# Row-wise infinity norm of an 8192x8192 matrix: issuing the loads from GpSimd instead of SP

## The chip, the cores and the metric

The kernel runs on one core of a Trainium2 chip. The metric is the device time of one execution in microseconds (us), as the median of several executions. A separate execution is taken with the hardware profiler; its views (busy times, waits, the chain of work that ended last, the timeline, DMA issues) are what the argument is read from.

The engines that matter here are VectorE (DVE), which does nearly all of the arithmetic, ScalarE (ACT) and GpSimd (POOL), which help with the last rows, and SyncE (SP), which in the kernel before does nothing but issue DMAs. "SPq" in a view is SP's instruction queue, where the DMA-issuing instructions stand.

## The reference

```python
def setup_inputs():
    return {"x": np.random.randn(8192, 8192).astype(np.float32)}

def reference(x):
    return np.linalg.norm(x, ord=np.inf, axis=1)
```

NumPy takes `axis=1` as "a vector norm for each row", so the result is, for each of the 8192 rows, the largest absolute value in it: 8192 floats. The input is 268.4 MB and is read exactly once; the output is 32 KB.

## The kernel before

**Tiling.** The 8192 rows are spread over the 128 partitions, 64 rows (R = 64) to a partition. `GROUPS = [46, 18]` (line 18) makes two groups, so that in the first each partition holds 46 neighbouring rows and in the second 18; within a group, what a partition reads is contiguous in memory. The work of a partition is therefore one long line of 64 x 8192 elements, which is cut into loads by column widths (lines 21 to 26): two loads of 8192 elements per partition (one row each, 4 MiB over all partitions), twenty-nine of 16384 (two rows, 8 MiB), one more of 16384 and one of 8192 that are shared out among engines, and then the last row in six pieces of 3920, 1984, 1040, 576, 320 and 352 elements. That is 33 entries in `WHOLE` and 6 in `LAST`, 39 loads in all.

**Buffers.** All loads but the very last go into one ring (line 54) of 3 x 16384 elements a partition, that is, three loads of full size. `load` (line 97) takes the next place in the ring, going back to 0 when the piece would not fit. So load u lies where load u-3 lay, and its DMA has to wait until the reduces that read load u-3 are done. By this rule the last full-size load (u = 31) lies in the ring where load 28 lay, and the load of 8192 together with the first five pieces of the last row lies where load 29 lay. The last piece has a buffer of its own, `last` (line 58), which also has columns for the partial results of the other pieces. The test on line 110 drops, for part of the loads, a dependency on the earlier load in the same place, which the reduce in between orders already; the change leaves it as it is.

**Engines.** `absmax` (line 67) is a VectorE reduce with absolute value; for a load of two rows it gives two results a partition at once. `shared` (line 85) splits a piece: VectorE reduces the first part, while ScalarE takes the absolute value of the rest in place and GpSimd reduces it as 32-bit integers (`max_pool`, line 72). It is used for the second row of load 31, for load 32 and for the first five pieces of the last row. At the end VectorE reduces `last`, pieces and partial results together (line 153), and SP stores the last column of results (line 154); ScalarE's queue stores the others (line 159).

**Order.** `keep` holds the instructions of an engine in the order in which the program gives them. Each engine has one in-order queue. In the kernel before every load is issued from SP's queue:

```python
        inst = nc.sync.dma_start(out=buf, in_=x_of[first[row]][:, a : a + w]).ins
```

SP has no other work until the last store, so what stands behind a load that waits for its place in the ring is only the next load. The program asks for each load just ahead of its use:

```python
    for u, (w, g) in enumerate(WHOLE):
        buf = load(pos, w)
```

SP however runs ahead of the other engines as far as the ring lets it: while load u is being reduced, loads u+1 and u+2 are already issued.

Of the kernel before, what the change touches and what calls it, by code (L numbers as in the profile page):

```python
# [1 line left out]

# [4 lines left out]

P = 128
FP32 = mybir.dt.float32
INT32 = mybir.dt.int32  # L10
MAX = mybir.AluOpType.max
X = mybir.AxisListType.X
ABS = mybir.ActivationFunctionType.Abs

GROUPS = [46, 18]


WHOLE = (
    [(8192, ())] * 2 + [(16384, ())] * 29 + [(16384, (3712, 3680)), (8192, (2016, 1984))]
)
LAST = [
    (3920, (1680,)), (1984, (848,)), (1040, (432,)), (576, (240,)), (320, ()), (352, ())
]
RING = 3 * 16384


@with_exitstack  # L30
def kernel(
    ctx: ExitStack,
    tc: tile.TileContext,
    x: bass.AP,
    out: bass.AP,
):
    nc = tc.nc
    n_rows, n_cols = x.shape
    R = n_rows // P
    assert R == sum(GROUPS) and n_cols == 8192  # L40
    keep = tc.keep_in_program_order


    first = []
    x_of, out_of = {}, {}
    for k in GROUPS:
        f = len(first)
        x_of[f] = x[f * P : (f + k) * P].rearrange("(p r) m -> p (r m)", r=k)
        out_of[f] = out[f * P : (f + k) * P].rearrange("(p r) -> p r", r=k)
        first += [f] * k  # L50

    single = ctx.enter_context(tc.tile_pool(name="single", bufs=1))

    ring = single.tile([P, RING], FP32)
    res = single.tile([P, R], FP32)

    n_parts = sum(1 + len(g) for w, g in LAST[:-1])
    last = single.tile([P, LAST[-1][0] + n_parts], FP32)

    def not_before(inst, other, why):  # L60
        tc.add_manual_dep(
            inst.ins, other.ins.name,
            mybir.DependencyInfo(mybir.DependencyClass.Sync, mybir.DependencyReason.DATA),
            reason=why,
        )

    def absmax(dst, src):
        return keep(nc.vector.tensor_reduce(  # L68
            out=dst, in_=src, axis=X, op=MAX, apply_absolute_value=True,
        ))  # L70

    def max_pool(dst, src):

        pool = nc.gpsimd
        keep(pool.add_instruction(  # L75
            mybir.InstTensorReduce(
                name=nc.get_next_instruction_name(),
                ins=[pool.lower_ap(src.bitcast(INT32))],
                outs=[pool.lower_ap(dst.bitcast(INT32))],
                op=MAX,  # L80
                axis=X,
            )
        ))

    def shared(part, buf, g):

        a = buf.shape[1] - sum(g)
        red = absmax(part[:, :1], buf[:, :a])
        for i, c in enumerate(g):
            keep(nc.scalar.activation(buf[:, a : a + c], buf[:, a : a + c], ABS))  # L90
            max_pool(part[:, 1 + i : 2 + i], buf[:, a : a + c])
            a += c
        return red

    loads = []

    def load(pos, w):

        row = pos // n_cols
        a = pos - first[row] * n_cols  # L100
        if pos + w == R * n_cols:
            buf = last[:, :w]
        else:
            at = loads[-1][0] + loads[-1][1] if loads else 0
            if at + w > RING:
                at = 0
            buf = ring[:, at : at + w]
        inst = nc.sync.dma_start(out=buf, in_=x_of[first[row]][:, a : a + w]).ins  # L108
        if pos + w < R * n_cols:
            if (len(loads) + 4) % 10 < 5:  # L110


                for b, v, earlier in loads:
                    if b < at + w and at < b + v:
                        tc.declare_no_dep(
                            inst, earlier, reason="ordered by the reduces in between",
                        )
            loads.append((at, w, inst))
        return buf


    pos = 0
    for u, (w, g) in enumerate(WHOLE):
        buf = load(pos, w)
        row, k = pos // n_cols, w // n_cols
        pos += w
        whole = k - 1 if g else k
        if whole:
            red = absmax(
                res[:, row : row + whole],  # L130
                buf[:, : whole * n_cols].rearrange("p (c m) -> p c m", m=n_cols),
            )
        if g:
            part = single.tile([P, 1 + len(g)], FP32, name=f"part{u}")
            shared(part, buf[:, whole * n_cols :], g)
            max_pool(res[:, row + whole : row + k], part)
        if u == 1:

            not_before(
                keep(nc.scalar.activation(res[:, :1], res[:, :1], ABS)),  # L140
                red, "not before the second row is in",
            )


    n = LAST[-1][0]
    for h, (w, g) in enumerate(LAST[:-1]):
        buf = load(pos, w)
        pos += w
        shared(last[:, n : n + 1 + len(g)], buf, g)
        n += 1 + len(g)  # L150

    load(pos, LAST[-1][0])
    absmax(res[:, R - 1 :], last)
    final = nc.sync.dma_start(out=out_of[first[-1]][:, GROUPS[-1] - 1 :], in_=res[:, R - 1 :])


    for f, o in out_of.items():
        k = min(o.shape[1], R - 1 - f)
        early = keep(nc.scalar.dma_start(out=o[:, :k], in_=res[:, f : f + k]))
        tc.add_manual_dep(  # L160
            early.ins, final.ins.name,
            mybir.DependencyInfo(
                mybir.DependencyClass.NoSync, mybir.DependencyReason.SCHED_ONLY
            ),
            reason="takes the later semaphore",
        )


# [1 line left out]
_INS = ['x']  # L170
_OUTS = [((8192,), 'float32')]


# [23 lines left out]
```

## Time and profile before

| | |
|---|---|
| Median of 5 executions | 627.45 us (627.35 to 627.52) |
| The profiled execution's own time | 627.55 us |
| Its span, first to last instruction | 625.8 us |
| VectorE busy | 536.7 us in 40 instructions |
| ScalarE busy | 15.0 us in 10 |
| GpSimd busy | 14.1 us in 14 |
| HBM read | 268.44 MB, 429 GB/s over the span |

The span counts from the first to the last instruction of the core; 1.75 us of the execution's own time lie outside it. Busy times leave out the instructions that issue DMAs. An engine's idle time is listed with what ended it (`<-`). "us to landing" is the time from the instruction that issues a DMA to the arrival of its last semaphore update, so it includes the time that the DMA stood behind earlier ones. "ring<-in_x_dram" is a load into the ring, "res" the tile of results, "part" and "last" the tiles of partial results. The lines of the profile stand in the prediction.

### The profile page before, as it was taken

The numbers are of one execution on the slowest core, as the hardware profiler recorded it, in microseconds if no ns is written. First come the engines' busy times: TensorE is split into PE (matmuls) and PEld (weight loads), VectorE is DVE, ScalarE is ACT, GpSimd is POOL, SyncE is SP. The second block draws the span as 40 slices with busy tenths as digits, with TensorE's granted clock in tenths as the row PEclk, the third lists the DMA queues.
The fourth block names the chain that finished last, engine by engine and source line by source line (L and its number), as shares of the span: only waits on it lengthen the run. The fifth ranks groups of instructions, "written<-read, shape, count | busy, mean of one in ns | idle before, by whom it ended". The sixth has DMA issues, their size and how long they took to land.

```text
span 625.8 us, 175 instructions
## 1 busy us (share of the span) xinstructions
DVE 536.7 (86%) x40; ACT 15.0 (2%) x10; POOL 14.1 (2%) x14
## 2 busy tenths in 40 slices
DVE  1938988889888899888898888988889888899888
ACT  0000000000000000000000000000000000000044
POOL 0000000000000000000000000000000000000026
DMA  8999999999999999999999999999999999999997
GB/s 369 436 469 402 469 402 469 402 469 402 469 402 448 423 415 457 402 469 402 469 402 469 402 469 402 469 402 461 411 423 448 406 465 402 469 402 469 402 436 304
DMA packets 6049, 268.47 MB, mean 429 GB/s; under 512 B 1057, under 2 KB 1313, under 8 KB 1697
## 3 DMA queue, kind: packets, MB, share of 16 engines
q1 hardware_dynamic: 5760, 268.44, 99.3%
q10 hardware_dynamic: 288, 0.03, 0.0%
q14 instruction: 1, 0.00, 0.0%
HBM read 268.44 MB, written 0.03 MB: 429 GB/s over the span
## 4 chain that ended last, share of the span: by engine, by line
DMA 71%; DVE 28%; SPq 0%; issue 0%; DVEq 0%
DMA ring<-in_x_dram 71%; DVE res L68 28%; DVE last L68 1%; SPq L108 0%; DVEq L68 0%
## 5 line engine op out<-in xcount | busy, mean ns | idle before, releaser
L68 DVE TENSOR_REDUCE res<-ring 128x2 f32<-128x16384 f32 (+1 forms) x32 | 525.4, 16420 | 86.4 <-DMA ring<-in_x_dram 86.4
L90 ACT ACTIVATE ring<-ring 128x3712 f32<-128x3712 f32 (+7 forms) x8 | 13.6, 1719 | 577.3 <-DMA ring<-in_x_dram 574.0
L75 POOL TENSOR_REDUCE part<-ring 128x1 int32<-128x3712 int32 (+3 forms) x4 | 10.1, 2561 | 607.7 <-ACT ring L90 607.7
L68 DVE TENSOR_REDUCE part<-ring 128x1 f32<-128x800 f32 (+1 forms) x2 | 5.5, 2748 | 0.1
L68 DVE TENSOR_REDUCE last<-ring 128x1 f32<-128x2240 f32 (+4 forms) x5 | 5.3, 1117 | 0.2 <-DMA ring<-in_x_dram 0.2
L75 POOL TENSOR_REDUCE last<-ring 128x1 int32<-128x1680 int32 (+3 forms) x4 | 3.4, 854 | 0.6 <-ACT ring L90 0.4
L140 ACT ACT_TABLE_LOAD x1 | 1.3, 1283 | 0.7 <-PEq L181 0.7
L140 ACT ACTIVATE res<-res 128x1 f32<-128x1 f32 x1 | 0.2, 203 | 29.3 <-DVE res L68 29.3
L68 DVE TENSOR_REDUCE res<-last 128x1 f32<-128x361 f32 x1 | 0.5, 530 | 0.1
L75 POOL TENSOR_REDUCE res<-part 128x1 int32<-128x3 int32 x2 | 0.4, 197 | 0.1
L181 POOL MEMSET const-float32-0.0<- 128x1 f32 x1 | 0.1, 98 | 0.2 <-issue 0.2
L181 POOL MEMSET const-uint8-127<- 128x1 uint8 x1 | 0.1, 102 | 0.0
L181 POOL MEMSET const-bfloat16-1.0<- 128x1 bf16 x1 | 0.1, 101 | 0.0
L181 POOL MEMSET const-float32-1.0<- 128x1 f32 x1 | 0.1, 98 | 0.0
## 6 DMA issues: line engine op xcount, KB each, us to landing
ring<-in_x_dram SPq DMA_DIRECT2D x3, 4096.0 KB, 21.4
ring<-in_x_dram SPq DMA_DIRECT2D x1, 1960.0 KB, 35.5
ring<-in_x_dram SPq DMA_DIRECT2D x1, 992.0 KB, 37.4
ring<-in_x_dram SPq DMA_DIRECT2D x1, 520.0 KB, 38.2
ring<-in_x_dram SPq DMA_DIRECT2D x30, 40.8
ring<-in_x_dram SPq DMA_DIRECT2D x1, 288.0 KB, 38.4
last<-in_x_dram SPq DMA_DIRECT2D x1, 176.0 KB, 38.3
ring<-in_x_dram SPq DMA_DIRECT2D x1, 160.0 KB, 38.4
```

Source lines behind the costliest of these rows:

```text
L68: return keep(nc.vector.tensor_reduce(out=dst, in_=src, axis=X, op=MAX, apply_absolute_value=True,))
L75: keep(pool.add_instruction(mybir.InstTensorReduce(name=nc.get_next_instruction_name(), ins=[pool.lower_ap(src.bitcast(INT32))], outs=[poo ...
L90: keep(nc.scalar.activation(buf[:, a : a + c], buf[:, a : a + c], ABS))
L140: keep(nc.scalar.activation(res[:, :1], res[:, :1], ABS)),
L181: nc = _bacc.Bacc("TRN2", target_bir_lowering=False, num_devices=1)
```

## The change

Only the first load stays on SP. All others, 38 DMAs, are issued from GpSimd's queue, with `keep`, so that they stand in the program's order among GpSimd's own instructions. The loads are asked for through `load_up_to`: during the two-row loads one at a time, as before; from the first entry that is shared among engines (u = 31, whose `g` is not empty) all that are left are asked for at once, so that they stand in GpSimd's queue ahead of its first reduce. Widths, ring places, reduces, the split among engines and the stores are the same.

```diff
-        inst = nc.sync.dma_start(out=buf, in_=x_of[first[row]][:, a : a + w]).ins
+        queue = nc.gpsimd if loads else nc.sync
+        inst = keep(queue.dma_start(out=buf, in_=x_of[first[row]][:, a : a + w])).ins
...
+    widths = [w for w, _ in WHOLE + LAST]
+    bufs = []
+
+    def load_up_to(n):
+        while len(bufs) < n:
+            bufs.append(load(sum(widths[: len(bufs)]), widths[len(bufs)]))
+
+
     pos = 0
     for u, (w, g) in enumerate(WHOLE):
-        buf = load(pos, w)
+        load_up_to(len(widths) if g else u + 1)
+        buf = bufs[u]
...
-    for h, (w, g) in enumerate(LAST[:-1]):
-        buf = load(pos, w)
-        pos += w
+    for buf, (w, g) in zip(bufs[len(WHOLE) :], LAST[:-1]):
         shared(last[:, n : n + 1 + len(g)], buf, g)
         n += 1 + len(g)
 
-    load(pos, LAST[-1][0])
     absmax(res[:, R - 1 :], last)
```

## The prediction, made before the change was run

> **What bounds the kernel now.** I read first the page's strip of 40 slices, its count of packets and its table of DMA queues, because the kernel reads 268 MB and does little with it.
>
> ```profile
> DVE  1938988889888899888898888988889888899888
> ...
> DMA  8999999999999999999999999999999999999997
> ...
> DMA packets 6049, 268.47 MB, mean 429 GB/s; under 512 B 1057, under 2 KB 1313, under 8 KB 1697
> ...
> q1 hardware_dynamic: 5760, 268.44, 99.3%
> ```
>
> The DMA engines are busy in every slice but the first and the last, and the packets of one queue, SP's, fill 99.3% of the time of 16 engines. VectorE has about a tenth of its time free. The 5760 packets tell the shape of a descriptor: 39 loads of 128 data packets and 16 semaphore writes are 5616, and the last store adds 144. So a row of a two-row load goes as one packet of 64 KB.
>
> Then the stretches of 58 us (three two-row loads each) in the table by windows, whose last two columns are the DMA share and GB/s:
>
> ```profile
> 42.00:100.00 58.00, 51.58 (x4) 0.00 (x0) 0.00 (x0) 1.00 1.00 434
> ...
> 506.00:564.00 58.00, 51.66 (x3) 0.00 (x0) 0.00 (x0) 1.00 1.00 434
> ```
>
> The rate is 434 GB/s from 42 to 564 us without a dip. The trace's packet records say why: a 64 KB packet takes 2,420 ns on its engine (median of 3840), a 32 KB one 1,213. A two-row load is 8 such packets on each of 16 engines, 8 x 2,420 = 19.36 us, and loads land 19.35 us apart. Nothing is left between them. The difference of the two sizes, 1,207 ns for 32,768 B, is 27.1 GB/s an engine; what is left over is about 6 ns a packet, and the small packets of the last pieces (1,280 B in 55 ns, 4,160 B in 161) say 8.
>
> Third, how much room an issue has, from the chain that ended last (start, duration) and the DMA issues:
>
> ```profile
> 59.16 40.81 DMA ring<-in_x_dram
> ...
> 99.99 17.23 DVE res L68
> ...
> 117.23 40.79 DMA ring<-in_x_dram
> ```
>
> ```profile
> ring<-in_x_dram SPq DMA_DIRECT2D x30, 40.8
> ```
>
> The chain looks as if VectorE held 28% of the path. It doesn't: a load issued at 117.23, when its ring place came free, lands at 158.02, but its own data needs 19.35 us of that. It stood behind other loads until 158.02 - 19.35 = 138.67. So every issue may be late by 138.67 - 117.23 = 21.4 us before the engines run dry.
>
> Last, the end, in the timeline:
>
> ```profile
> 581.73 2.70 SPq L108 DMA_DIRECT2D ring<-in_x_dram  x6
> 584.47 0.43 SPq L108 DMA_DIRECT2D last<-in_x_dram  x1
> ...
> 606.64 6.48 POOL L75 TENSOR_REDUCE part<-ring 128x1 int32<-128x3712 int32 x2 [606.20 <-ACT ring L90]
> ...
> 617.59 5.29 DVE L68 TENSOR_REDUCE last<-ring 128x1 f32<-128x2240 f32 x5 [0.16 <-DMA ring<-in_x_dram]
> ```
>
> SP issues the last seven loads in 3.2 us, when the reduce of load 29 has ended. GpSimd's first reduce starts 22 us later. From 617.59 VectorE sets the end: five reduces without a gap, then the last one and a store.
>
> **What the Trainium skill says.** "DMA: Bandwidth & Descriptors", section "Issuing engines are not separate DMA queues": DMAs from SP, ACT and GpSimd end on the same 16 engines and interleave; another issuer saves only sequencer time. The trace agrees as far as it goes: with one queue the engines are full, and SP's 0.33 us an issue is nowhere on the path.
> Same page, "Latency and other measured facts": the first byte comes after about 1 us from GpSimd, where software makes the descriptors, and 0.6 us from SP; engines 7 and 15 are usually slower, for which the descriptor rings that GpSimd's DMAs keep in SBUF are a best guess. No GpSimd DMA is in this trace, so it shows neither.
> "SBUF — State Buffer", section "Who interferes with whom": GpSimd can't write descriptors while VectorE holds the shared ports, but on trn2 a `tensor_reduce` never takes them. All of VectorE's 40 instructions are such reduces, so no starvation is to be expected. The trace has the two engines side by side at 606.64 and after: GpSimd's reduce of 3712 takes 3,282 ns there and ScalarE's pass over as many 3,297, as if VectorE weren't there.
>
> **The change part by part.** The sum is made against the profiled execution, 627.55 us (span 625.8 and 1.75 around it); the median, 627.45, is 0.10 lower.
>
> *SP's 38 issues go.* 38 x 0.33 us = 12.5 us of SP's queue, all under DMA time: 0.
>
> *GpSimd issues 38 DMAs.* I price one at the page's 1 us; from below SP's 0.33, from above 3 us, three times the page. In the middle of the kernel one load comes up every 19.35 us and has 21.4 us of room: 0 even at 3 us. Behind a waiting load stands only the next load, and nobody waits for that. Without the room each microsecond would be paid 29 times.
>
> *The first rows.* SP issues row 0 at 0.74 us as before, so the first byte moves at the same time. GpSimd's four memsets end at 0.44 and the start barrier at about 0.7, so row 1 is in by 1.8 us, loads 2 and 3 by 3.8 (9.8 at the upper price). Row 0 alone keeps the engines busy until its landing at 12.85: no gap. But rows 0 and 1 are now in two queues and share the engines. Row 0 lands between 12.85 and 22.56, at worst with row 1. Then VectorE reduces two rows of 8.69 us, until 22.56 + 17.4 = 39.9 instead of 31.25, still before load 2 lands at 41.9. Load 4, which takes their places, is issued at 40 to 41 instead of 31.3, and must be there when load 3 is through, at 41.9 + 19.35 = 61.2: 20 us of room. 0.
>
> *The end.* Load 31 becomes free to go at 562.4 as before. Seven loads follow at 581.73 and take 7 x 1 = 7 us on GpSimd (2.3 to 21), until 588.7. Two loads are ahead of them: load 30 lands at 583.8 and load 31 at about 603.2, so load 32 has 20 us to be issued, and every later one has its predecessors' transfer more. These loads wait for VectorE's reduce of load 29 only, never for GpSimd's or ScalarE's work, so standing ahead of GpSimd's reduces makes no circle. The reduces, due at 606.64, are free 18 us earlier. At 3 us an issue GpSimd would be free at 602.7, still in time. 0.
>
> *The closing.* GpSimd now has DMAs to account for at the end; the last lands near 622 and the span ends at 625.8. I take 0.1 us, from 0 to 0.5.
>
> *The transfers themselves.* This is the only part that can count. 264.2 of 268.4 MB move by another kind of descriptor: 252 packets of 64 KB (or their equivalent) on each engine, at 2,420 ns. Each nanosecond a packet is 0.25 us. From below: if the fixed 8 ns vanished, -252 x 8 ns = -2.0 us. From above, the page's section "Measured (HBM→SBUF, 128 partitions, SWDGE, issued from GpSimd)" gives 425 GB/s for its largest transfer against the trace's 434: 264.2 MB x (1/425 - 1/433.5) = +12.2 us. I take 0, because the engine is the same, the bytes are 99.7% of a packet's time, and some 2 loads of descriptors lie ready ahead of the engines.
>
> Sum: 0 + 0.1 on the median 627.45, 627.5 us.
>
> **The rivals.**
> *Slower by the descriptors' way:* an engine has to fetch its descriptors from a ring in SBUF, and the slowest of the 16 sets each load's landing. Place: every packet from row 1 on. Price: at the page's 425 GB/s 627.55 + 12.2 = 639.7 us. It decides from 5 ns a packet, which is 1.25 us or 0.2% (about what a measurement of this kernel can tell from no change). For it: the DMA has no spare time at all, so any loss is paid in full. Against: 64 KB for each descriptor leaves 2.4 us to fetch the next.
> *Slower by cut descriptors:* if GpSimd's software makes shorter ones out of a 64 KB row, the last pieces show the price. 15,680 B take 585 ns, 1.0% more a byte than the long ones: +6 us, 634. 7,936 B take 302, 3% more: +19 us, 646. 4,160 B take 161, 4.8% more: +30 us, 657. Nothing in the trace speaks for it but that all 64 KB packets seen are SP's.
> *Faster:* the fixed time of a packet shrinks. All of it is 2.0 us, 625.5. Half, 626.5, would not leave the 0.2%.
> *The change does nothing it says:* GpSimd's queue starts late. Only over 10 us at the start, or 20 later, would count; the prices are a tenth of that.
>
> **How the numbers follow.** No change 0.57 (own range 626.5 to 628.6), faster by over 0.2% 0.13 (towards 625.3), slower by the descriptors' way 0.18 (629 to 640), cut descriptors 0.12 (634 to 657). So faster 0.13, same 0.57, slower 0.30. The range goes from 625.3 to 640: it leaves out the longer half of the cut descriptors and a little at both ends, some 0.1 to 0.15.
>
> **What would show it.** In the profile after: a second queue of loads beside SP's with about 5,500 packets, 64 KB ones at 2,420 ns, and 434 GB/s from 42 to 564 us. The first reduce starts nearer 22 than 13 us, and the third still at 41.9. GpSimd's first reduce starts at 606.6. I am wrong if the middle stretches show less than 433 GB/s or more packets than that (a rival on the transfers), if VectorE's idle time before a two-row reduce differs from 2.13 us, or if the start or the end shows a stretch without DMA.

## The result and the profile after

The changed kernel takes 628.84 us (median of 22 runs, 628.71 to 629.26), the kernel before 627.47 (40 runs, 627.35 to 627.66): a ratio of 1.0023, 95% interval 1.0017 to 1.0029. That is 1.37 us more. The kernel is slower, at the edge of what the prediction counted as no change: its 0.2% lie inside the interval, the range that it gave to that likeliest case ends 0.24 us below the measured time, and the whole range holds it. The profiled execution takes 628.82 us with a span of 627.0.

The strip, the packets and the queues of the changed kernel:

```profile
DVE  0778988889988889888898888988889988889887
...
DMA  8999999999999999999999999999999999999996
...
DMA packets 5809, 268.48 MB, mean 428 GB/s; under 512 B 1056, under 2 KB 1056, under 8 KB 1456
...
q0 software_dynamic: 5232, 264.24, 97.4%
q1 hardware_dynamic: 288, 4.19, 1.7%
...
q14 instruction: 1, 0.01, 0.0%
```

The loads moved to a queue of software descriptors, q0, and the engines are as full as before. The new queue has fewer packets than the 38 x (128 + 16) = 5,472 that 128 data packets and 16 semaphore writes for each DMA would give, because short rows are joined: four rows of 1,280 B go as one packet of 5,120. The row of q14, the instruction queue, has 0.01 MB, one packet of 8 KB at 616.7 us. In the kernel before, its one packet had 24 B:

```profile
q14 instruction: 1, 0.00, 0.0%
```

The 8 KB look like nothing, and are a third of the loss.

The stretches of 58 us, with the DMA share and GB/s at the end:

```profile
42.00:100.00 58.00, 51.60 (x4) 0.00 (x0) 1.59 (x3) 1.00 1.00 434
...
506.00:564.00 58.00, 51.66 (x3) 0.00 (x0) 1.59 (x3) 1.00 1.00 434
```

The rate is 434 GB/s as before, and the packet records agree: a 64 KB packet of the software queue takes 2,422 ns (median; the slowest of 3840 is 2,434), the same as SP's in the kernel before (2,422). The 1.59 us of GpSimd in each stretch are three issues of 0.53.

The start and the end, from the timeline. First two lines of the kernel before, then the changed kernel:

```profile
12.85 8.69 DVE L68 TENSOR_REDUCE res<-ring 128x1 f32<-128x8192 f32 x1 [12.85 <-DMA ring<-in_x_dram]
...
41.91 17.22 DVE L68 TENSOR_REDUCE res<-ring 128x2 f32<-128x16384 f32 x1 [10.66 <-DMA ring<-in_x_dram]
```

```profile
0.74 0.37 SPq L109 DMA_DIRECT2D ring<-in_x_dram  x1
1.25 1.74 POOL L109 DMA_DIRECT2D ring<-in_x_dram  x3 [0.80 <-PEq L199]
20.09 17.28 DVE L68 TENSOR_REDUCE res<-ring 128x1 f32<-128x8192 f32 x2 [20.09 <-DMA ring<-in_x_dram]
...
41.87 17.22 DVE L68 TENSOR_REDUCE res<-ring 128x2 f32<-128x16384 f32 x1 [4.50 <-DMA ring<-in_x_dram]
...
606.54 6.48 POOL L75 TENSOR_REDUCE part<-ring 128x1 int32<-128x3712 int32 x2 [20.97 <-ACT ring L90]
...
618.05 5.22 DVE L68 TENSOR_REDUCE last<-ring 128x1 f32<-128x2240 f32 x5 [0.74 <-DMA ring<-in_x_dram]
```

The first reduce starts at 20.09 instead of 12.85, the third at 41.87 against 41.91: sharing the engines at the start costs nothing. GpSimd's first reduce starts when it did. But the first of the six pieces of the last row ("the first piece" from here on) lets VectorE start at 618.05 instead of 617.59, and VectorE waits 0.74 us for it instead of 0.16. This is "the lag" below.

The other two thirds of the loss are in the closing, the instructions with which each engine ends the program: SP waits for the semaphores of the loads and stores, each engine has DRAIN instructions, and GpSimd and SP then exchange signals (the barrier). Instructions that only synchronise appear in the view of a source line: here the line that closes the program, with the least, median and longest duration in ns and the starts of the first and the last. First the kernel before, then the changed one:

```profile
L192 POOLq DRAIN  x3: 34/83/484, 622.4 to 625.5; - x3
```

```profile
L199 SPq EVENT_SEMAPHORE  x8: 17/28/28, 624.3 to 627.0; - x8
...
L199 POOLq DRAIN  x3: 40/102/3612, 622.7 to 626.8; - x3
```

GpSimd's first closing DRAIN takes 3,612 ns instead of 484. It starts beside GpSimd's last reduce and ends at 626.28; SP, which was the last to be ready in the kernel before, was ready at 625.60. The instruction records of the two executions give the budget of the span, in us:

```
                                        before     after     difference
VectorE's last reduce starts            622.97    623.37     +0.40
SP ready (its own closing DRAIN)        625.08    625.60     +0.52   (0.12 more: two more waits)
GpSimd takes the barrier                625.12    626.33     +1.21   (0.69 more: its DRAIN)
end of the span                         625.78    627.04     +1.26   (0.05 more)
```

So 0.40 us go by before VectorE's last reduce, and 0.86 after it. What lies around the span is the same, 1.77 and 1.78.

### The profile page after: what moved, and what is told of

Same layout as the page of the kernel before. It is cut to its first block, busy times and chain, and to the rows that moved or that the text cites. A ratio compares the mean times of both kernels' runs of the same rounds, so it can differ in the third digit from the quotient of the medians.

```text
span 627.0 us, 176 instructions
## 1 busy us (share of the span) xinstructions
DVE 536.5 (86%) x40; ACT 15.1 (2%) x10; POOL 34.3 (5%) x52
## 4 chain that ended last, share of the span: by engine, by line
DMA 76%; DVE 23%; issue 0%; another core or an unknown queue 0%; POOL 0%; DVEq 0%; PEldq 0%
DMA ring<-in_x_dram 76%; DVE res L68 22%; DVE last L68 1%; POOL ring L109 0%; DVEq L68 0%; PEldq L199 0%
## 5 line engine op out<-in xcount | busy, mean ns | idle before, releaser
L109 POOL DMA_DIRECT2D ring<-in_x_dram x37 | 19.7, 535 | 564.9 <-DVE res L68 564.0
```

What stands on the lines that cost most here:

```text
L109: inst = keep(queue.dma_start(out=buf, in_=x_of[first[row]][:, a : a + w])).ins
```

## The experiments

Theory, from these traces: the transfers cost nothing. The loss is (a) GpSimd's closing DRAIN, which goes through the DMAs that GpSimd has issued, (b) an instruction fetch on one DMA engine, which GpSimd's longer stream needs, and (c) SP's two more waits. For (c) the other traces are enough: from the start of VectorE's last reduce to SP's readiness 2.11 to 2.12 us pass in the kernels in which SP has 6 closing semaphore instructions (as in the kernel before), 2.18 with 7, 2.24 with 8 (as in the changed one) and 2.24 to 2.27 with 9; with 10 it is 2.30 to 2.44 in three kernels and 2.12 in one (`pool_24`). Rivals: any use of GpSimd's DMAs has a fixed closing; the late pieces belong to software descriptors; it costs to issue from an engine with work of its own at the end. Each time below is a median beside runs of the kernel before on the same chip, which took 627.43 to 627.48. Differences of a few tenths between kernels are read from profiles, since most of the intervals of the ratios hold 1. Each profile is one execution, and executions of one kernel can differ by some tenths too (`drain_early`, below, took from 627.84 to 628.59 us).

**How the closing grows: 19, 19 and 1 load on GpSimd.** Three kernels change one line; `pool_late`, `pool_early` and `pool_one` in this order:

```diff
-        queue = nc.gpsimd if loads else nc.sync
+        queue = nc.gpsimd if len(loads) >= 20 else nc.sync
...
+        queue = nc.gpsimd if 0 < len(loads) < 20 else nc.sync
...
+        queue = nc.gpsimd if len(loads) == 1 else nc.sync
```

> SP issues loads 0 to 19, GpSimd the last 19. Theory: GpSimd's closing DRAIN costs about 0.082 us for each DMA that GpSimd has issued ((3.612 - 0.484) / 38), and the lag of the last pieces comes from an instruction fetch of GpSimd's longer stream. Then the DRAIN takes 0.48 + 19 x 0.082 = 2.0 us and ends before SP's own closing, the fetch at 616.7 us is gone because GpSimd's stream is shorter, and what stays is SP's two more closing waits: 627.5 us. Rival 1, any use of GpSimd's DMAs costs a fixed closing: DRAIN 3.6 us, about 628.2. Rival 2, the lag of the last pieces belongs to GpSimd's descriptors: first piece still lands near 618.0, 627.9 us.

> GpSimd issues loads 1 to 19, SP row 0 and the last 19. Theory (each DMA ever issued counts in the DRAIN): DRAIN 2.0 us as in the kernel with the last 19 on GpSimd, hidden; 627.5 us. Rival, only DMAs still recent or uncleared count: DRAIN 0.5 us, also hidden, the same time. Rival, a fixed closing: DRAIN 3.6 us, 628.2 us.

> One load (row 1) on GpSimd, all others on SP. Theory: DRAIN 0.48 + 0.08 = 0.57 us, no fetch in the tail, 627.5 us. Rival, a fixed closing for any GpSimd DMA: DRAIN 3.6 us, 628.2 us.

Measured: 627.90 (ratio 1.0007, 0.9998 to 1.0015), 629.37 (1.0034, 1.0021 to 1.0046) and 627.56 us (1.0001, 0.9993 to 1.0010). The DRAINs, one kernel a fence in this order:

```profile
L199 POOLq DRAIN  x3: 40/108/2061, 622.2 to 625.6; - x3
```

```profile
L199 POOLq DRAIN  x3: 34/99/2056, 624.2 to 627.5; - x3
```

```profile
L199 POOLq DRAIN  x3: 34/99/578, 622.3 to 625.5; - x3
```

With 0, 1, 19 and 38 DMAs the DRAIN takes 484, 578, 2,061 and 3,612 ns: 82 ns for each. It counts every DMA that GpSimd has issued: nineteen that had landed over 230 us before cost as much as the last nineteen. A fixed closing is out. With up to 19 the DRAIN ends before SP is ready and costs nothing. In `pool_late` no 8 KB are fetched in the span, and the last pieces come in early on GpSimd's queue:

```profile
617.40 5.28 DVE L68 TENSOR_REDUCE last<-ring 128x1 f32<-128x2240 f32 x5 [0.15 <-DMA ring<-in_x_dram]
```

At 617.40 it is earlier than in the kernel before (617.59), so the lag does not belong to software descriptors. The 627.90 us are more than the 627.5 expected. Of the 0.42 us over the kernel before, 0.16 lie around the span (1.94 us in the median of the runs, 1.78 before), and 0.3 in it (626.0 against 625.7 in the medians), of which the profiled execution, at 625.85, shows only a part. Its cause stays open.

`pool_early` missed by 1.9 us for a reason that none of the theories had: at load 20 the queue changes, and the loads on both sides of the change share the engines. Load 19 lands at 390.25 instead of 370.9 (the landing of load 18 plus 19.35), VectorE then runs 137 us without a gap to catch up, and the first piece is reduced from 619.36. The change from SP to GpSimd in `pool_late` delays load 19 by 16.8 us, and that fits into the room of 21.4.

The records of the landings show where the two part. Each load makes 16 updates of its semaphore. In `pool_late` all 16 of load 19 come between 387.35 and 387.70; in `pool_early` three come by 387.7 and the other 13 between 389.86 and 390.25, about one packet of 64 KB later. So load 22, which takes the place of load 19, is issued at 407.52 instead of 405.24, while the last packets of load 21 end between 408.6 and 409.1. From 409 to 410 us the packets fill only 0.66 of the engines' time, the one microsecond between 340 and 560 in which they fill less than 0.9, and the landings from load 22 on are 1.7 to 2.0 us later than those of `pool_late`. Why load 19's last packet came later on 13 engines in one direction only was not tried.

**The fetch, moved.** In the changed kernel, forty memsets that nothing needs on GpSimd, early:

```diff
+        if u == 3:
+            pad = single.tile([P, 1], FP32, name="pad")
+            for _ in range(40):
+                keep(nc.gpsimd.memset(pad, 0.0))
```

> The changed kernel with 40 tiny memsets of a scratch column on GpSimd after its first loads, while it has nothing to do. They move the point of GpSimd's stream at which the instruction fetch happened some 40 instructions earlier. Theory: the 8 KB fetch leaves 616.7 us for about 250 us; it still takes 0.3 us from one DMA engine that has no spare time, so the lag of that engine stays to the end and the time stays at 628.8 us. Rival, only a fetch in the tail counts: first piece lands at 617.6, 628.4 us. Rival, the lag has nothing to do with the fetch: 628.8 with the lag in place but no engine behind in the middle.

Measured: 628.96 us (1.0024, 1.0015 to 1.0033). The fetch moved from 616.7 to 237.2 us. The lag stayed: load 31 is reduced from 603.60 instead of 603.08, and the first piece from here:

```profile
617.99 5.28 DVE L68 TENSOR_REDUCE last<-ring 128x1 f32<-128x2240 f32 x5 [0.16 <-DMA ring<-in_x_dram]
```

What is lost at 237 us is still missing 380 us later. The semaphore updates show it load by load: the last of the 16 comes 0.56 us after the first in load 12, which lands at 235.5 us, and 0.97 in load 13, and it stays at 0.97 to 1.02 to the end, while the last but one stays within 0.61. So one engine alone falls behind at the fetch and never catches up; none of them has spare time. The memsets themselves, from 3.0 to 9.1 us, leave no such mark. In all eight kernels whose fetch falls among the loads the distance grows at the fetch and stays, by 0.25 to 0.48 us. Ahead of it, it differs from execution to execution (0.33 to 0.65).

The next kernel was meant to avoid the fetch with a shorter stream:

```diff
-            if (len(loads) + 4) % 10 < 5:
+            if True:
```

> The changed kernel with the dependency on the earlier load in the same place dropped for all loads, not for half of them (the reduce in between orders them): some 12 waiting instructions fewer on GpSimd, the same 38 DMAs. Theory: the fetch happens at the 71st of GpSimd's instructions, which now comes after 622 us, so no engine lags while loads run; first piece lands near 617.5, DRAIN still 3.6 us but starts 0.4 earlier: 628.4 us. Rival, the lag belongs to GpSimd's descriptors: first piece at 618.0, 628.8 us.

Measured: 628.79 us (1.0022, 1.0013 to 1.0030). It missed: GpSimd has 98 recorded instructions instead of 88, because without these dependencies there are more waits (24 instead of 14 at the loads), not fewer. So the fetch came earlier, at 587.7, and the first piece is reduced from 617.71, between the two cases. The DRAIN is 3,611 ns and starts 0.14 us earlier, and the span is 0.14 us shorter.

**The fetch by itself, and another queue.** The kernel before, all loads on SP, with 64 memsets on GpSimd in the middle:

```diff
+        if u == 10:
+            pad = single.tile([P, 1], FP32, name="pad")
+            for i in range(64):
+                m = keep(nc.gpsimd.memset(pad, 0.0))
+                if i == 0:
+                    not_before(m, red, "in the middle of the loads")
```

> The kernel before, all loads on SP, with 64 tiny memsets of a scratch column on GpSimd after the reduce of load 10. They carry GpSimd's stream past its 71st instruction in the middle of the loads. Theory: one 8 KB instruction fetch near 220 us, one engine behind from there to the end, load 31 and the first piece land 0.3 to 0.55 us later than before, and nothing else changes: 627.9 us. Rival, a fetch does nothing unless it falls in the last pieces, or only with GpSimd's descriptors: 627.4 us.

Measured: 627.81 us (1.0005, 0.9997 to 1.0014) against 627.43. Its profile has the row of q14 and the late first piece, with all loads still in SP's queue:

```profile
q1 hardware_dynamic: 5760, 268.44, 99.3%
...
q14 instruction: 1, 0.01, 0.0%
```

```profile
617.93 5.29 DVE L68 TENSOR_REDUCE last<-ring 128x1 f32<-128x2240 f32 x5
```

VectorE's last reduce starts 0.35 us later than in the kernel before, and the span is 0.35 us longer. So (b) costs some 0.4 us also when SP issues the loads. The record of a fetch does not name the engine that it is for; that is read from the counts (the last column has the recorded instructions of an engine's stream that started before the fetch):

```
kernel            fetch (8 KB) at   takes     recorded instructions passed
changed               616.7 us      315 ns    GpSimd 70
sp_fetch              225.2         309       GpSimd 74
pad                   237.2         309       GpSimd 69
no_waits              587.7         313       GpSimd 72
row1_halves           616.5         309       GpSimd 71
drain_early           616.9         309       GpSimd 70
row1_sp               623.5         315       GpSimd 68
pool_29               622.8         433       GpSimd 70
pool_24               626.6         549       GpSimd 69 (all; after the span)
act                   590.4         309       ScalarE 56, GpSimd 10
pool_late             none                    GpSimd 63 in all
before                none                    GpSimd 36 in all
```

Wherever the fetch falls, GpSimd has passed 68 to 74 recorded instructions, and without a fetch it has at most 63; in `act`, where it has passed only 10, ScalarE's stream is the long one.

ScalarE in GpSimd's place:

```diff
+        queue = nc.scalar if loads else nc.sync
...
+        load_up_to(len(widths) if g else max(4, u + 1))
```

> The changed kernel with ScalarE's queue in GpSimd's place (first four loads asked for ahead of ScalarE's first instruction). Theory: closing and fetch are GpSimd's own, so another queue with work of its own at the end, but with hardware descriptors, costs nothing: 627.5 us. Rival, issuing from an engine that also works at the end costs: 628 us or more.

Measured: 627.97 us (1.0008, 1.0000 to 1.0017), not the 627.5 expected, and it looks like the rival. The profile says otherwise: ScalarE's stream has grown too, and 8 KB are fetched at 590.4. The first piece is reduced from 618.01, as late as in the changed kernel, and the closing DRAIN is 484 ns again. Issuing from a busy engine by itself shows no cost; VectorE's last reduce starts 0.42 us later than before, and the span is 0.41 us longer: what is lost is lost where the fetch's lag is seen, and nothing comes after it.

**The closing, taken out.** GpSimd's reduces of the last row's pieces are dropped from the changed kernel, so that its DRAIN begins earlier (the kernel leaves these shares of the last row out of the maximum):

```diff
+    keep(nc.vector.memset(last[:, LAST[-1][0] :], 0.0))
...
-        shared(last[:, n : n + 1 + len(g)], buf, g)
+        shared(last[:, n : n + 1 + len(g)], buf, g, pool=False)
```

> The changed kernel without GpSimd's four reduces of the pieces of the last row (their columns of the partial results are set to 0 at the start; the shares of the last row that GpSimd reduced are left out of the maximum). GpSimd's last instruction ends at 618.7 instead of 623.1, and its closing DRAIN is reached from 616.7 on. Theory: the DRAIN goes through its 38 entries one after the other and only has to wait for the last loads to land at 623.0, so it ends near 623.2, hidden; the closing's 0.7 us is gone, the fetch's lag stays: 628.1 us. Rival, the DRAIN takes its 3.1 us after the last load has landed: 628.8 us.

Measured: 628.13 us (1.0012, 1.0005 to 1.0018), as expected: 0.7 less than the changed kernel. The profiled execution was the fastest, of 627.84, in which VectorE's last reduce started 0.28 earlier than in the changed kernel. But the DRAIN is not what was expected:

```profile
L201 POOLq DRAIN  x3: 40/102/5951, 618.6 to 625.8; - x3
```

It takes 5,951 ns from 618.60 and ends at 624.55, 1.6 us after the last load has landed (622.95), not 0.2. It is hidden, since SP is ready only at 625.32, and the 0.7 us are gone. What it does in detail while DMAs are still under way stays open.

**The start.** Row 1 on SP as well:

```diff
+        queue = nc.gpsimd if len(loads) > 1 else nc.sync
```

> The changed kernel with row 1 on SP as well, so that rows 0 and 1 do not share the engines. Theory: the start costs nothing, because load 2 sets the pace: the first reduce starts near 13 us again, the third still at 41.9, and the time is the changed kernel's less one DRAIN step of 0.08: 628.8 us. Rival, the sharing at the start costs some tenths: 628.3 us.

Measured: 635.57 us (1.0129, 1.0115 to 1.0143). Both expectations failed, by far. Its timeline and its windows:

```profile
27.30 8.69 DVE L68 TENSOR_REDUCE res<-ring 128x1 f32<-128x8192 f32 x1 [27.30 <-DMA ring<-in_x_dram]
56.36 25.81 DVE L68 TENSOR_REDUCE res<-ring 128x1 f32<-128x8192 f32 x2 [20.38 <-DMA ring<-in_x_dram]
```

```profile
62.00:82.00 20.00, 20.00 (x2) 0.20 (x1) 0.53 (x1) 1.00 0.85 354
```

Row 1 is there only at 56.36, so load 4, which takes the places of both rows, is issued at 65.3, when loads 2 and 3 are through (load 3 lands at 61.2). The 354 GB/s of the window from 62 to 82 us, instead of 434, tell the loss: no packet of a load is under way from 60.8 to 66.6 us, which is most of the 6.7 us, and VectorE works without a gap until 202 us before it waits for a load again. The Trainium skill, "DMA: Bandwidth & Descriptors", section "Queues, rings and completion order", says that an engine takes turns between its queues packet by packet. Rows 0 and 1 come in packets of 32 KB (1,213 ns) and the loads of the other queue in 64 KB (2,422), so SP gets a third: 8 turns of 3.63 us for row 0, 16 for row 1, from 1.75 us on, are 30.8 and 59.9 us at most. They were reduced from 27.3 and 56.4, about one turn earlier. To test it, loads 2 and 3 were issued in two halves, with packets of 32 KB:

```diff
+        if len(loads) in (2, 3):
+            h = w // 2
+            keep(queue.dma_start(out=buf[:, :h], in_=x_of[first[row]][:, a : a + h]))
+            inst = keep(queue.dma_start(out=buf[:, h:], in_=x_of[first[row]][:, a + h : a + w])).ins
```

> Rows 0 and 1 on SP, as in the kernel that took 635.57 us, but loads 2 and 3 on GpSimd in two halves each, so that their packets are 32 KB like those of the rows. Theory, the two queues take turns packet by packet whatever a packet's size: rows 0 and 1 land at about 20 and 41 us (1.75 + 16 and 32 packets of 1.213) instead of 27.3 and 56.4, places come free in time, nothing runs dry: 628.8 us. Rival, the queues share by bytes, or SP's queue is served worse for another reason: 635 us again.

```profile
20.17 8.69 DVE L68 TENSOR_REDUCE res<-ring 128x1 f32<-128x8192 f32 x1 [20.17 <-DMA ring<-in_x_dram]
39.60 25.81 DVE L68 TENSOR_REDUCE res<-ring 128x1 f32<-128x8192 f32 x2 [10.75 <-DMA ring<-in_x_dram]
```

Measured: 629.16 us (1.0028, 1.0017 to 1.0039), rows at 20.17 and 39.6 as the packets say. Both runs together fit turns by packets, and not by bytes: by an estimate from 434 GB/s, rows that got half of the bytes would have landed near 21 and 40 us in `row1_sp` too. In the changed kernel row 0 and row 1 stand at the heads of the two queues, both with packets of 32 KB.

**The point from which the DRAIN counts, and a try to beat both.** GpSimd issues the last 29, or the last 24:

```diff
+        queue = nc.gpsimd if len(loads) >= 10 else nc.sync
...
+        queue = nc.gpsimd if len(loads) >= 15 else nc.sync
```

> SP issues loads 0 to 9, GpSimd the other 29. Theory: DRAIN 0.484 + 29 x 0.0823 = 2.87 us, from 622.25 to 625.1, about where SP's own closing ends (625.0), so the closing is just hidden; GpSimd's stream is short enough for the fetch to come after the loads: 627.9 us, as with 19. Rival, the closing grows with each GpSimd DMA whether hidden or not: 628.3 us.

> SP issues loads 0 to 14, GpSimd the last 24; a try for the best of both. Theory: DRAIN 0.484 + 24 x 0.0823 = 2.46 us, hidden; no fetch among the loads; first piece lands near 617.4, VectorE's last reduce at 622.75 (0.2 earlier than in the kernel before); the last store has the last of SP's semaphores, so that no wait follows it: 627.3 us, 0.1 under the kernel before. Rival, the reset of more semaphores and SP's longer list of waits eat that: 627.8 us, as with 19 and 29 of GpSimd's loads.

Measured: 627.82 (1.0007, 0.9998 to 1.0015) and 627.90 us (1.0008, 0.9999 to 1.0016). The DRAINs, 29 first:

```profile
L199 POOLq DRAIN  x3: 40/108/2877, 622.2 to 625.7; - x3
```

```profile
L199 POOLq DRAIN  x3: 40/107/2467, 622.2 to 625.4; - x3
```

2,877 and 2,467 ns were worked out as 2,870 and 2,460. With 29 it ends at 625.06, just under SP's 625.17: about thirty DMAs are where it begins to show. The try failed all the same. VectorE's last reduce starts at 622.77, 0.20 earlier than before, and SP is ready at 624.88, 0.20 earlier; but from GpSimd's last DRAIN to its last signal 0.52 us pass where it was 0.16, and the span ends at 626.01 instead of 625.78. What holds the signal back is not shown: an 8 KB fetch, at 626.6, comes only after the last record of the span. No version here beats the kernel before.

## Why the prediction was right or wrong

The measured time lies in the stated range partly by luck. The range goes up to 640 for two rivals on the transfers, and neither occurred; what made the kernel slower was one term that was not in the sum and one whose upper bound was too low.

- **The bound.** Right: the DMA engines set the pace of both kernels, at 434 GB/s.
- **The transfers, 0 taken, -2.0 to +12.2.** Right. 64 KB packets take the same 2,422 ns (the prediction wrote 2,420), with 2,434 for the slowest, and cut descriptors don't occur. The 425 GB/s of the Trainium skill's page "DMA: Bandwidth & Descriptors", section "Measured (HBM→SBUF, 128 partitions, SWDGE, issued from GpSimd)", on which the slower rival stood, is not what this chip shows: 434. In the three kernels whose last loads are GpSimd's and that have no fetch among the loads, the first piece came 0.19 to 0.21 us sooner than in the kernel before. That the queue does this is not shown: the distance between the first and the last of a load's 16 updates is some 0.35 us in those three and 0.5 in the kernel before, but from 0.33 to 0.65 in the other kernels whose last loads are GpSimd's, ahead of their fetch.
- **GpSimd's issues, 1 us each.** They take 0.53 us, and there is room for them; the seven at the end are out by 585.6, ahead of the 588.7 worked out. 0, as said.
- **The start.** The cost is 0 as said, with row 0 reduced from 20.09 and load 4 issued at 37.66. But how much the margin depends on was not seen: it rests on two queues with equal packets, and `row1_sp` lost 6.7 us with what looks like a smaller change.
- **The end.** GpSimd's reduces start when they did. What was missing is that 38 DMAs and their waits also lengthen GpSimd's stream of instructions: 88 records instead of 36, past the point where 8 KB more of them are fetched. That term was not in the sum at all. VectorE's last reduce starts 0.40 us later than in the kernel before (0.60 later than in `pool_late`, which has no fetch).
- **The closing, 0.1 taken, 0 to 0.5.** This is the term that was mis-sized: 0.86 us. 0.12 are SP's two more waits, 0.69 the part of GpSimd's DRAIN that SP no longer hides, 0.05 what follows. The price was bounded as if only the last DMA had to be accounted for; the DRAIN takes 82 ns more for each of the 38.

Sum: 0.40 + 0.86 = 1.26 us of span, and 1.37 between the medians. The likeliest case had 0.1, and its own range (626.5 to 628.6) was missed by 0.24.

What stays open: what the DRAIN does while loads are under way; the last tenths of the kernels with 19, 24 and 29 late loads on GpSimd; why an engine falls behind by up to 0.48 us at a fetch of 0.31; and why, at a change from GpSimd to SP in the middle, 13 engines finish the last load of the old queue a packet later.

## What to carry to other kernels

When issues are moved to another engine, count what they leave behind there: the length of its instruction stream and what it has to settle at the end, both of which can come due on the path although every issue is hidden. In this kernel, whose DMA engines are always full, an 8 KB fetch delayed the end whether it fell at 225, 237, 588 or 617 us. Two queues that run side by side share by packets, so look at the size of a row on both before you split loads between them.

## What the runs showed of the hardware that was not expected

- GpSimd's closing DRAIN takes 82 ns more for every DMA that GpSimd has issued in the program (484, 578, 2,061, 2,467, 2,877, 3,529, 3,612 and 3,696 ns with 0, 1, 19, 24, 29, 37, 38 and 39), long finished ones included. Only where loads were still under way did it take longer (5,951 with 38).
- One 8 KB instruction fetch takes 0.31 us of one DMA engine while the engines are full. It came when GpSimd had passed 68 to 74 recorded instructions (ScalarE 56, in one kernel), and it put that engine 0.25 to 0.48 us further behind the others, to the end.
- The software queue joins short rows into packets of 2.8 to 5.1 KB, where SP's queue sends each row as its own packet.
- Two queues that take turns with packets of 32 and 64 KB share the engines 1 to 2.
